# A hybrid trunk on one core: blocks of four third and last, the first tile's products at once, gates spread into the last combination, router products in two halves of the array

## The chip, the cores and the metric

One core of a Trainium2 chip runs the whole program. The metric is the time of one execution on the device, in microseconds (us). The engines are TensorE (PE in the profile; PEld is its weight loading), VectorE (DVE), ScalarE (ACT), GpSimd (POOL) and SyncE (SP), whose queue issues nearly all loads.

## The reference

Two layers over 512 tokens of width 1024, batch 1, all in float32:

```python
for i in range(DEPTH):
    h = _rms_norm(x, norm_mix[i])
    z = h @ w_in[i]
    ...
    x = x + merged @ w_out[i]
    h2 = _rms_norm(x, norm_ffn[i])
    x = x + _hier_moe(h2, ...)
    g_ple = jax.nn.sigmoid(_rms_norm(x, norm_ple[i]) @ w_ple_gate[i])
    x = x + g_ple * (p[i] @ w_ple_proj[i])
return _rms_norm(x, norm_final)
```

Between `z` and `merged` stand dilated attention and a convolution branch. `_hier_moe` chooses one of 4 groups and then 2 of its 8 experts for each token; an expert is `(silu(x @ w_gate) * (x @ w_up)) @ w_down` with a hidden width of 512, and there are 32 of them, each with three matrices of 2 MB.

## The kernel before, in words

The tokens stand in four tiles of 128 rows, `self.x[0..3]`. A layer runs through four parts.

**Mixer.** Products with dense weights are made of three matmuls (`mm3`, L312 to L314): weights and activations are split into a high and a low part. A weight chunk of 128 x 1024 is loaded (`load_chunks`, L216), its high part is made by ScalarE (L234), its low part by GpSimd (L239), or, for the first four chunks and some others, half by GpSimd and half by VectorE (L237). `take(c)` sees to it that chunks up to `c + self.ahead` are split and chunks up to `c + self.look` are loaded. The part starts with the value projection, `tokens_b` over chunks v0 to v3: for each token tile t, `token_b` makes 8 x 3 matmuls (two k for each chunk). Ahead of that the tiles are normalized and transposed: `prep` multiplies x by the row's scale and a gain on VectorE and puts the transposition on the list `todo`; `split_T` transposes a tile on PE (L419), copies the high part on ScalarE (L424) and makes the low part on VectorE (L426). At the program's start (`run`) the loop over t does `rms`, `prep` and `split_chunks(t)`, and pops a transposition at t = 1 and t = 2; what is left is popped by `value`, behind each tile's products. Instructions of this opening are recorded under L102. Behind it come the convolution, attention and output products (ps_z, ps_ao, ps_wo).

**Router.** `route_tile` (one generator for each tile, interleaved with the output products) normalizes and transposes a tile (L832), makes its 36 logits as eight products of 128 x 128 into rows 0 to 35 of a PSUM tile (L841), copies them (L868), transposes them back (L873) and works out the chosen experts on VectorE (L881 to L924). `order_experts` counts tokens for each expert and ranks the 28 experts that are not static by that count.

**Experts.** Tokens are gathered into blocks of 128 slots; a block holds two experts of 64 slots or four of 32. `BLK` lists the blocks: 0 and 1 hold the static experts 0 to 3, the others hold experts by rank, the eight of lowest rank in two blocks of four. Stages c = 0 to 6 take two blocks each. A stage makes, on PE: gate and up products (ps_g, ps_u) of its two blocks, the down products (ps_y) of the blocks of the stage before, transposes (ps_hT), the gathering of the next stage's tokens (ps_xg) and the combination (ps_c) of the blocks two stages back, whose sums VectorE adds to x (L1150). Weights come in items of 512 KB, 384 of them a layer: four of each matrix of an expert. SP issues them (L252) in the order of `self.items`, which `Trunk.__init__` builds from BLK: for c from 1 on, gate and up items of blocks 2c and 2c+1, and, from c = 2, down items of blocks 2c-2 and 2c-1; the down items of blocks 12 and 13 end the list. They land in a ring of 45 slots, `s4`, that is shared with chunks and other rows; `pump` issues items as long as a stage's reserve (`KEEP`) stays free. Behind block 4's gate and up products stands the check for overflowing experts (`overflow`, L1291): a loop whose count is read from memory by every engine.

**Gate.** With the last combination (blocks 12 and 13), `then(t)` transposes tile t of x (L1266) and `first(t)` makes the products with the gate weights pg0 to pg3 (ps_tb). `rms` (squares on ScalarE, L384; a dozen operations on single columns, L392 to L401) and `gated` (tanh L1412, L1414, L1416) stand behind them, and the second half of the products and the next layer's normalization (L431) follow.

Of the kernel before, what the change touches and what calls it, by code (L numbers as in the profile page):

```python
# [8 lines left out]
F32 = mybir.dt.float32  # L9
# [3 lines left out]
AF = mybir.ActivationFunctionType  # L13
OP = mybir.AluOpType
# [3 lines left out]
T, D, P = 512, 1024, 128  # L18
NT = T // P
KD = D // P  # L20
H, HD = 8, 64
CW, CK = 512, 31
NG, NPG, NE = 4, 8, 32
# [3 lines left out]
CAP = 64  # L27
GS = 256


NST, NSM = 4, 8
NDY = NE - NST
LD = 4
BLK = ([(2 * i, 2 * i + 1) for i in range(NST // 2)]
       + [tuple(range(NST + 4 * i, NST + 4 * i + 4)) for i in range(NSM // 4)]
       + [(i, i + 1) for i in range(NST + NSM, NE, 2)])
NB = len(BLK)

# [41 lines left out]
AH = 4  # L80
LK = 5, 3
# [82 lines left out]
class Trunk:  # L164
# [198 lines left out]

    def tokens_b(self, cs, src, then):
        for c in cs:
            self.take(c)
        for t in range(NT):
            then(t, self.token_b(cs, src, t))

# [65 lines left out]
    def run(self):  # L435
# [6 lines left out]
        for t in range(NT):  # L442
            if t:
                nc.sync.dma_start(self.x[t], self.dr["x"][t * P:(t + 1) * P])
            self.load_chunks(t)
        self.small(0)
# [8 lines left out]
        for t in range(NT):  # L455
            n = self.s4.get(F32, "n")
            self.prep(t, gain, self.rms(t, n), n)
            if t in (1, 2):
                self.todo.pop(0)()
            self.split_chunks(t)  # L460
        self.nc = nc
# [29 lines left out]
    def mixer(self, l):  # L491
        nc = self.nc
        v, act = nc.vector, nc.scalar
        base = l * NCH
        self.look, self.ahead = LK[0], AH
        pos = self.pos = {s: base + i for i, s in enumerate(SEQ_CHUNKS)}
# [7 lines left out]
        def value(t, ps):  # L504
            act.activation(vt(t), ps, AF.Copy)
            self.ps.free()
            if self.todo:
                self.todo.pop(0)()
        self.tokens_b([pos[f"v{i}"] for i in range(4)], self.hT, value)

        if l:
            self.load_c2()
# [296 lines left out]
    def route_init(self):  # L809
        self.nh = [[None] * NT for _ in range(2)]  # L810
        self.lgw, self.Ew, self.lgT = (self.s2.get(F32, n) for n in ("lgw", "Ew", "lgT"))
        self.Mb = self.tn(128, "Mb", BF)
        self.spos8, self.base8, self.slots8 = (self.tn(2 * NT, n) for n in ("sp", "sb", "sl"))
# [8 lines left out]
    def route_tile(self, t):  # L822
# [16 lines left out]
        def logits(h):  # L839
            for k in range(4 * h, 4 * h + 4):  # L840
                pe.matmul(pl[0:36, 0:P], self.gwr[:, k * 36:(k + 1) * 36], nT[h][:, k % 4 * P:(k % 4 + 1) * P],  # L841
                          start=k == 0, stop=k == KD - 1)
            self.s2.free()
# [22 lines left out]
        logits(1)  # L866
        lgT = self.lgT[0:36, t * P:(t + 1) * P]
        act.activation(lgT, pl[0:36, 0:P], AF.Copy)  # L868
        self.ps.free()
        for _ in range(LAGS[2]):  # L870
            yield
        pl = self.ps.get(F32, "lg")
        pe.transpose(pl[:, 0:36], lgT, self.cc(C_ID, P)[0:36, 0:36])  # L873

# [57 lines left out]
    def order_experts(self):  # L932

        v = self.nc.vector
        cnt = self.posb[:, 128:160]
        key, rank, small, base, self.cnt, top, rest, bs = (self.lgT[:, 32 * i:32 * i + 32] for i in range(8))
        bs, ss = bs[:, :8], bs[:, 8:16]
        over = lambda a, n: a.unsqueeze(1).to_broadcast([P, n, 32])
# [18 lines left out]
        v.tensor_scalar(small, rank, float(NSM), 32.0, op0=OP.is_lt, op1=OP.mult)  # L957
        v.scalar_tensor_tensor(base, rank, float(NSM - 1), small, op0=OP.subtract, op1=OP.mult)
        v.scalar_tensor_tensor(base, rank, float(CAP), base, op0=OP.mult, op1=OP.subtract)
        if CAP * NST != CAP // 2 * NSM:  # L960
            v.tensor_scalar(base, base, float(CAP * NST - CAP // 2 * NSM), None, op0=OP.add)
        v.tensor_copy(base[:, :NST], self.cc(C_BASE, NST))
# [70 lines left out]
    def moe(self, l):  # L1033
# [219 lines left out]
        cs = [self.pos[f"pg{i}"] for i in range(4)]  # L1253
        self.pg = []

        def first(t):
            self.pg.append(self.token_b(cs, self.src, t))

        def then(t):
# [11 lines left out]
            self.gT[0].append(hi)  # L1271
            self.gT[1].append(lo)
            if t:
                first(t - 1)
        combine((NB - 2, NB - 1), then)
        first(NT - 1)
        for t in range(NT):
            junk = self.s4.get(F32, "j")
            r = self.rms(t, junk)
            self.s4.free()  # L1280
            h_ = self.tn(1, f"rh{t}")
            v.tensor_scalar(h_, r, 0.5, None, op0=OP.mult)
            self.rh.append(h_)

# [116 lines left out]


    def ple(self, l):
        nc = self.nc
# [4 lines left out]

        def gated(t, h, ps):  # L1410
            th = self.s2.get(F32, "th")
            self.last = act.activation(th, ps, AF.Tanh, scale=self.rh[t]).ins  # L1412
            self.ps.free()
            v.scalar_tensor_tensor(th, th, 1.0, self.pp[h](t), op0=OP.add, op1=OP.mult)  # L1414
            xs = self.x[t][:, h * T:(h + 1) * T]
            self.last_v = v.tensor_add(xs, xs, th).ins  # L1416
            self.s2.free()

        for t in range(NT):
            gated(t, 0, self.pg[t])  # L1420
        self.pp[0].free()
# [136 lines left out]
```

## Time and profile before

| | us |
|---|---|
| median of 3 runs | 1818.47 (1818.14 to 1821.3) |
| the profiled execution | 1818.76 |
| its span, first to last instruction | 1817.0 |
| TensorE busy | 1720.2 |
| VectorE busy | 874.1 |
| ScalarE busy | 540.2 |
| GpSimd busy | 380.7 |

The mean granted clock of TensorE was 0.986 of full speed, and the DMA engines moved 478.66 MB. The profile's page gives busy times, the span in slices and the costliest groups of instructions; the trace behind it gives timelines of an engine, the chain of waits (what released each step, followed back from the end), waits by engine, and busy times in any stretch. Layer 0 lasts to about 912 us, layer 1 from there on.

### The profile page before, as it was taken

The page shows a single profiled execution, that of the slowest core. Times are in us where ns is not written, and L with a number is a line of the kernel's source. Part 1 is how long each engine was busy: PE and PEld are TensorE (multiplying, and loading weights), DVE is VectorE, ACT ScalarE, POOL GpSimd, SP SyncE. Part 2 cuts the span into 40 slices and gives each one's busy share as a digit, 9 for nine tenths or more (in the row PEclk, how much of TensorE's full clock was granted, in tenths as well). Part 3 has the DMA queues.
Part 4 walks back from the last instruction along what each step waited for, and adds up shares of the span by engine and source line. Part 5 has one row for each costly group of instructions (what it writes and reads, how often), then busy time and mean ns, then how long its engine had stood idle before and what let it go on. Part 6 is the DMA issues. An engine that isn't in the chain of part 4 may idle for free.

```text
span 1817.0 us, 24202 instructions
## 1 busy us (share of the span) xinstructions
PE 1720.2 (95%) x8324; PEld 1050.6 (58%) x8324; DVE 874.1 (48%) x2131; ACT 540.2 (30%) x1041; POOL 380.7 (21%) x203
## 2 busy tenths in 40 slices
PE   5999999998989999998999999998989899999997
PEld 4777787753244355444777777877514344355356
DVE  5688864572042243223648888537601332343146
ACT  4355534221011012103545554433201011022145
POOL 3445424300200001001444454252002000010021
PEclk9999999999999999999999999999999999999999
DMA  5222236389989999996242212564899899999931
GB/s 228 83 68 71 82 135 236 121 318 387 419 337 419 419 419 416 413 419 275 90 132 70 70 58 70 197 220 174 328 398 419 335 418 419 419 417 419 420 153 47
DMA packets 133616, 478.66 MB, mean 263 GB/s; under 512 B 14832, under 2 KB 15344, under 8 KB 133488
## 3 DMA queue, kind: packets, MB, share of 16 engines
q1 hardware_dynamic: 133488, 477.06, 67.5%
q8 instruction: 68, 1.11, 0.2%
q14 instruction: 60, 0.49, 0.1%
HBM read 474.90 MB, written 2.10 MB: 263 GB/s over the span
## 4 chain that ended last, share of the span: by engine, by line
PE 64%; DMA 20%; DVE 7%; issue 4%; ACT 2%; POOL 1%; SPq 0%; POOLq 0%; DVEq 0%; ACTq 0%
DMA s_w<-wdn 10%; PE ps_g L102 8%; PE ps_y L102 7%; DMA s_w<-wu 6%; PE ps_u L102 6%; PE ps_z L312 6%; PE ps_z L313 6%; PE ps_z L314 6%; PE ps_xg L102 5%; PE ps_c L102 5%; DMA s_w<-wg 3%; PE ps_tb L312 2%; PE ps_tb L313 2%; PE ps_tb L314 2%; PE ps_O L691 1%
## 5 line engine op out<-in xcount | busy, mean ns | idle before, releaser
L239 POOL TENSOR_TENSOR s_lo<-s_raw,s_hi 128x1024 fp32r<-128x1024 f32 x114 | 275.8, 2431 | 811.7 <-ACT s_hi L234 422.7
L102 PE MATMUL ps_u<-s_w,s_xg 128*64 128x512 f32 (+1 forms) x1024 | 240.1, 595 | 12.5 <-DMA s_w<-wu 12.1
L102 PE MATMUL ps_g<-s_w,s_xg 128*64 128x512 f32 (+1 forms) x1024 | 223.4, 603 | 14.2 <-DMA s_w<-wdn 9.3
L102 PE MATMUL ps_y<-s_w,s_hT 128*64 128x512 f32 (+1 forms) x1024 | 223.7, 601 | 11.3 <-DMA s_w<-wdn 10.7
L313 PE MATMUL ps_z<-s_hTl,s_hi 128*128 128x512 f32 x512 | 203.3, 397 | 0.0
L312 PE MATMUL ps_z<-s_hTh,s_hi 128*128 128x512 f32 x512 | 200.1, 391 | 0.0
L314 PE MATMUL ps_z<-s_hTh,s_lo 128*128 128x512 f32 x512 | 199.7, 390 | 0.0
L102 PEld LDWEIGHTS ps_u<-s_w,s_xg 128*64 128x64 f32 (+1 forms) x1024 | 67.7, 130 | 179.3 <-issue 117.3
L102 PEld LDWEIGHTS ps_y<-s_w,s_hT 128*64 128x64 f32 (+1 forms) x1024 | 69.6, 131 | 162.7 <-issue 113.8
L102 PEld LDWEIGHTS ps_g<-s_w,s_xg 128*64 128x64 f32 (+1 forms) x1024 | 64.8, 131 | 160.5 <-issue 127.6
L525 DVE SCALAR_TENSOR_TENSOR s_acc<-ps_z,smt,s_acc 128x511 f32<-128x511 f32 (+27 forms) x210 | 153.8, 732 | 4.6
L234 ACT ACTIVATE s_hi<-s_raw 128x1024 fp32r<-128x1024 f32 x120 | 125.5, 1057 | 8.6 <-PE ps_wo L313 4.2
L1105 DVE SCALAR_TENSOR_TENSOR s_h<-s_h,ps_g 128x512 f32<-128x512 f32 x28 | 19.2, 687 | 210.4 <-ACT s_h L1104 204.0
L1104 ACT ACTIVATE s_h<-ps_g,rs 128x512 f32<-128x512 f32 x28 | 19.2, 686 | 328.4 <-PE ps_g L102 287.7
L1150 DVE TENSOR_TENSOR s_x<-s_x,ps_c 128x512 f32<-128x512 f32 x112 | 75.2, 685 | 79.9 <-PE ps_c L102 47.4
L313 PEld LDWEIGHTS ps_z<-s_hTl,s_hi 128*128 128x128 f32 x512 | 96.2, 188 | 21.9 <-issue 3.1
L312 PEld LDWEIGHTS ps_z<-s_hTh,s_hi 128*128 128x128 f32 x512 | 96.1, 188 | 21.1 <-issue 1.0
L314 PEld LDWEIGHTS ps_z<-s_hTh,s_lo 128*128 128x128 f32 x512 | 96.2, 188 | 19.6 <-issue 0.8
L102 PE MATMUL ps_xg<-s_OH,s_xh 128*128 128x256 f32 x412 | 102.6, 290 | 3.7 <-DVE s_lgT L941 3.7
L1115 ACT ACTIVATE s_hT<-ps_hT 128x512 f32<-128x512 f32 x28 | 15.4, 596 | 300.3 <-PE ps_hT L102 300.3
L102 PE MATMUL ps_xg<-s_OH,s_xl 128*128 128x256 f32 x412 | 101.3, 286 | 0.0
L1106 DVE TENSOR_TENSOR s_h<-s_h,ps_u 128x512 f32<-128x512 f32 x28 | 19.3, 688 | 156.6 <-PE ps_u L102 156.6
(274 smaller groups left out, 2769.8 us busy)
## 6 DMA issues: line engine op xcount, KB each, us to landing
s_w<-wu SPq DMA_DIRECT2D x256, 512.0 KB, 9.9
s_w<-wdn SPq DMA_DIRECT2D x256, 512.0 KB, 9.9
s_w<-wg SPq DMA_DIRECT2D x248, 512.0 KB, 9.9
s_raw<-wd SPq DMA_DIRECT2D x124, 512.0 KB, 3.4
s_w<-wg SPq DMA_DIRECT2D x16, 256.0 KB, 7.4
s_x<-x SPq DMA_DIRECT2D x4, 512.0 KB, 9.9
out<-s_n SPq DMA_DIRECT2D x8, 256.0 KB, 2.0
s_gain<-gains SPq DMA_DIRECT2D x3, 512.0 KB, 3.8
```

The costliest lines, as they stand in the source:

```text
L102: i = f(*a, **k)
L234: nc.scalar.activation(hi, raw, AF.Copy)
L239: nc.gpsimd.tensor_tensor(lo, raw, hi.bitcast(F32), op=OP.subtract)
L312: mm(out, lh, rh, start=start, stop=False)
L313: mm(out, lh, rl, start=False, stop=False)
L314: mm(out, ll, rh, start=False, stop=stop)
L525: v.scalar_tensor_tensor(o, i, w, o, op0=OP.mult, op1=OP.add)
L691: nc.tensor.matmul(ps[64 * hh:64 * hh + 64, j * P:T], vt(j, (2 * p + hh) * HD, (2 * p + hh + 1) * HD), src, start=j == 0, stop=j == 3)
L1104: act.activation(t, pg, AF.Tanh, scale=rh[p])
L1105: v.scalar_tensor_tensor(t, t, 1.0, pg, op0=OP.add, op1=OP.mult)
L1106: v.tensor_mul(t, t, pu)
L1150: v.tensor_add(xs, xs, ps)
```

## The change

- `BLK`: block 2 holds four experts (ranks 0 to 3), blocks 3 to 12 two each, block 13 four (ranks 4 to 7). `order_experts` computes the base slots for this numbering with three more operations on 128 x 32 elements. Stage 1 has then 48 items of gate and up instead of 64, stage 2 loads 24 down items instead of 32, and the last stage loads 16 + 32 gate and up items and 16 + 24 down items.
- Start: tile 0's transposition is popped in the loop at t = 0; those of tiles 1 to 3 are popped by a hook in the middle (after k = 3) of the tile before. Chunks 0, 2, 3 are split by tiles 0, 1, 2, and in layer 0's value projection `ahead` is 1 instead of `AH`.
- Router: products of even k go to rows 0 to 35, those of odd k to rows 64 to 99 of the PSUM tile, that is to two halves of the array's columns; two copies take them out, and two accumulating products with columns of the identity, instead of one transposition, add and transpose them. Rows 32 to 63 of `lgT` are zeroed once a layer.
- Gate: `rms` of tile t moves into `then(t)`, the first half's `gated` into `first(t)`, behind tile t's products.

```diff
-BLK = ([(2 * i, 2 * i + 1) for i in range(NST // 2)]
-       + [tuple(range(NST + 4 * i, NST + 4 * i + 4)) for i in range(NSM // 4)]
-       + [(i, i + 1) for i in range(NST + NSM, NE, 2)])
+BLK = ([(2 * i, 2 * i + 1) for i in range(NST // 2)] + [tuple(range(NST, NST + 4))]
+       + [(i, i + 1) for i in range(NST + NSM, NE, 2)] + [tuple(range(NST + 4, NST + NSM))])
...
-    def tokens_b(self, cs, src, then):
+    def tokens_b(self, cs, src, then, hook=None):
...
-            then(t, self.token_b(cs, src, t))
+            then(t, self.token_b(cs, src, t, hook))
...
-            if t in (1, 2):
+            self.split_chunks((0, 2, 3, 3)[t])
+            if t == 0:
                 self.todo.pop(0)()
-            self.split_chunks(t)
...
-        self.look, self.ahead = LK[0], AH
+        self.look, self.ahead = LK[0], AH if l else 1
...
-            if self.todo:
+            if l and self.todo:
                 self.todo.pop(0)()
-        self.tokens_b([pos[f"v{i}"] for i in range(4)], self.hT, value)
-
+        halves = []
+
+        def middle():
+            halves.append(0)
+            if not l and len(halves) % KD == KD // 2 and self.todo:
+                self.todo.pop(0)()
+        self.tokens_b([pos[f"v{i}"] for i in range(4)], self.hT, value, middle)
+
+        self.ahead = AH
...
+        self.nc.gpsimd.memset(self.lgT[32:64, :], 0.0)
...
-                pe.matmul(pl[0:36, 0:P], self.gwr[:, k * 36:(k + 1) * 36], nT[h][:, k % 4 * P:(k % 4 + 1) * P],
-                          start=k == 0, stop=k == KD - 1)
+                o = k % 2 * 64
+                pe.matmul(pl[o:o + 36, 0:P], self.gwr[:, k * 36:(k + 1) * 36], nT[h][:, k % 4 * P:(k % 4 + 1) * P],
+                          start=k < 2, stop=k >= KD - 2)
...
-        lgT = self.lgT[0:36, t * P:(t + 1) * P]
-        act.activation(lgT, pl[0:36, 0:P], AF.Copy)
+
+        halves = [slice(64 * i, 64 * i + 36) for i in range(2)]
+        lgT = self.lgT[:, t * P:(t + 1) * P]
+        for a in halves:
+            act.activation(lgT[a], pl[a, 0:P], AF.Copy)
...
-        pe.transpose(pl[:, 0:36], lgT, self.cc(C_ID, P)[0:36, 0:36])
+        for i, a in enumerate(halves):
+            pe.matmul(pl[:, 0:36], lgT[0:100], self.cc(C_ID, P)[0:100, a], start=i == 0, stop=i == 1)
...
-        v.scalar_tensor_tensor(base, rank, float(NSM - 1), small, op0=OP.subtract, op1=OP.mult)
+
+        v.tensor_scalar(bs32, rank, 4.0, -40.0, op0=OP.is_ge, op1=OP.mult)
+        v.scalar_tensor_tensor(bs32, bs32, -11.0, rank, op0=OP.add, op1=OP.add)
+        v.tensor_mul(base, bs32, small)
...
-        self.pg = []
-
         def first(t):
-            self.pg.append(self.token_b(cs, self.src, t))
+            self.gated(t, 0, self.token_b(cs, self.src, t))
...
             self.gT[1].append(lo)
+            junk = self.s2.get(F32, "j")
+            r = self.rms(t, junk)
+            self.s2.free()
+            h_ = self.tn(1, f"rh{t}")
+            v.tensor_scalar(h_, r, 0.5, None, op0=OP.mult)
+            self.rh.append(h_)
             if t:
                 first(t - 1)
```

The loop over t with `rms` behind `first(NT - 1)` and the one with `gated(t, 0, ...)` at the head of `ple` are gone; `gated` itself is the same.

Three places of the order. First ScalarE at the start of the program, one piece of the difference; s_n_131 and s_n_149 are tile 1's squares in the one and the other order, ps_tr_149 and ps_tr_131 tile 0's transposes.

```order
-L102 ACTIVATE s_n_131,ss_1_132<-s_x_68 128x512
-L102 ACTIVATE s_n_131,ss_1_134<-s_x_68 128x512
-L102 ACTIVATE s_hTh_100<-ps_tr_149 128x2x128
-L102 ACTIVATE s_hTh_101<-ps_tr_149 128x2x128
-L102 ACTIVATE s_hTh_102<-ps_tr_158 128x2x128
-L102 ACTIVATE s_hTh_103<-ps_tr_158 128x2x128
+L102 ACTIVATE s_hTh_100<-ps_tr_131 128x2x128
+L102 ACTIVATE s_hTh_101<-ps_tr_131 128x2x128
+L102 ACTIVATE s_hTh_102<-ps_tr_140 128x2x128
+L102 ACTIVATE s_hTh_103<-ps_tr_140 128x2x128
+L102 ACTIVATE s_n_149,ss_1_150<-s_x_68 128x512
+L102 ACTIVATE s_n_149,ss_1_152<-s_x_68 128x512
```

Tile 1's squares moved behind the four copies of tile 0's transposes.

Second PE in the last stage of layer 0, where block 12 ends (ps_u) and block 13 begins (ps_g). Before:

```order
L102 MATMUL ps_u_6218<-s_w_6027,s_xg_6058 64x512
L102 MATMUL ps_g_6327<-s_w_6033,s_xg_6057 64x512
L102 MATMUL ps_g_6327<-s_w_6035,s_xg_6057 64x512
L102 MATMUL ps_g_6327<-s_w_6033,s_xg_6057 64x512
L102 MATMUL ps_g_6327<-s_w_6035,s_xg_6057 64x512
```

With the change:

```order
L102 MATMUL ps_u_6134<-s_w_5934,s_xg_5974 64x512
L102 MATMUL ps_g_6243<-s_w_5940,s_xg_5973 32x512
L102 MATMUL ps_g_6243<-s_w_5951,s_xg_5973 32x512
L102 MATMUL ps_g_6243<-s_w_6139,s_xg_5973 32x512
L102 MATMUL ps_g_6243<-s_w_6141,s_xg_5973 32x512
```

Block 13 takes four items (s_w) of four experts in turn, 32 slots each, where it took two of two experts.

Third VectorE in the last combination of layer 0, from the first half of tile 1's sum (s_x_3970 before, s_x_3909 after) on. Before:

```order
L1150 TENSOR_TENSOR s_x_3970<-s_x_3970,ps_c_6638 128x512
L237 TENSOR_TENSOR s_lo_6590<-s_raw_6521,s_hi_6589 128x512
L1268 TENSOR_TENSOR s_gTl_6609<-ps_tr_6610,s_gTh_6608 128x512
L1268 TENSOR_TENSOR s_gTl_6609<-ps_tr_6617,s_gTh_6608 128x512
L1150 TENSOR_TENSOR s_x_3970<-s_x_3970,ps_c_6644 128x512
```

With the change:

```order
L1168 TENSOR_TENSOR s_x_3909<-s_x_3909,ps_c_6669 128x512
L392 TENSOR_SCALAR rms_6655<-ss_0_6651 128x1
L1168 TENSOR_TENSOR s_x_3909<-s_x_3909,ps_c_6675 128x512
L237 TENSOR_TENSOR s_lo_6602<-s_raw_6517,s_hi_6601 128x512
L394 TENSOR_SCALAR rms_6655<-ss_0_6653,rms_6655 128x1
L396 TENSOR_SCALAR rms_6655<-rms_6655 128x1
L397 TENSOR_SCALAR rms_6655<-rms_6655 128x1
L1284 TENSOR_TENSOR s_gTl_6621<-ps_tr_6622,s_gTh_6620 128x512
L1284 TENSOR_TENSOR s_gTl_6621<-ps_tr_6629,s_gTh_6620 128x512
```

The second half of tile 1's sum moved ahead of the split (L237), and the root mean square of tile 0 stands between.

## Rows read from the trace of the kernel before

**Rows 1.** Page, busy time by engine: us (share) x instructions.
```profile
PE 1720.2 (95%) x8324; PEld 1050.6 (58%) x8324; DVE 874.1 (48%) x2131; ACT 540.2 (30%) x1041; POOL 380.7 (21%) x203
```

**Rows 2.** Busy times by stretch; the last columns are clock, DMA share, GB/s.
```profile
core 0: us, PE busy (x) PEld busy (x) DVE busy (x) ACT busy (x) POOL busy (x), PEclk, DMA share, GB/s
50.00:260.00 210.00, 208.85 (x976) 162.15 (x976) 165.72 (x321) 105.35 (x208) 93.11 (x55) 1.00 0.21 69
425.00:485.00 60.00, 51.68 (x198) 9.22 (x191) 4.68 (x11) 1.37 (x2) 3.83 (x2) 1.00 1.02 411
530.00:535.00 5.00, 0.61 (x4) 0.00 (x0) 0.69 (x1) 0.00 (x0) 0.00 (x0) 1.00 0.67 274
540.00:545.00 5.00, 5.00 (x26) 1.72 (x24) 0.13 (x1) 0.69 (x1) 0.00 (x0) 1.00 1.01 402
550.00:555.00 5.00, 5.00 (x46) 1.38 (x46) 0.95 (x2) 0.00 (x0) 0.00 (x0) 1.00 1.03 421
760.00:830.00 70.00, 67.95 (x344) 35.02 (x341) 17.78 (x32) 13.80 (x26) 0.00 (x0) 1.00 1.03 419
830.00:840.00 10.00, 10.00 (x39) 6.91 (x40) 5.72 (x9) 0.00 (x0) 0.00 (x0) 0.85 1.02 419
```

**Rows 3.** Timeline of SP's queue, layer 0's last stage: start us, us, what.
```profile
750.12 9.12 SPq L252 DMA_DIRECT2D s_w<-wg  x8
...
791.34 39.15 SPq L252 DMA_DIRECT2D s_w<-wdn  x32
```

**Rows 4.** Page, DMA issues: count, KB each, us from issue to landing.
```profile
s_w<-wdn SPq DMA_DIRECT2D x256, 512.0 KB, 9.9
```

**Rows 5.** Chain of waits, 755 to 865 us: start us, us, what.
```profile
763.43 7.67 PE ps_xg L102 x64
...
778.37 5.44 PE ps_pe L102 x24
...
811.43 13.73 PE ps_y L102 x64
...
829.61 8.46 PE ps_c L102 x29
838.06 13.93 PE ps_y L102 x64
```

**Rows 6.** Timeline of SP's queue, layer 1's last stage.
```profile
1685.39 39.65 SPq L252 DMA_DIRECT2D s_w<-wdn  x32
```

**Rows 7.** Chain of waits, 1690 to 1750 us.
```profile
1732.38 13.94 PE ps_y L102 x64
```

**Rows 8.** Timeline of PE at the start; in brackets idle before and releaser.
```profile
10.68 1.94 PE L419 MATMUL ps_tr<-c,s_n 128*128 128x128 f32 x8 [10.68 <-DVE s_n L102]
17.88 1.94 PE L419 MATMUL ps_tr<-c,s_n 128*128 128x128 f32 x8 [5.26 <-DVE s_n L102]
...
23.98 1.10 PE L419 MATMUL ps_tr<-c,s_n 128*128 128x128 f32 x8
...
34.74 0.80 PE L313 MATMUL ps_tb<-s_lo,s_hTh 128*128 128x512 f32 x1 [2.25 <-DVE s_lo L102]
...
48.69 0.39 PE L312 MATMUL ps_z<-s_hTh,s_hi 128*128 128x512 f32 x1
```

**Rows 9.** Chain of waits, 5 to 52 us.
```profile
15.61 2.13 DVE s_n L102
```

**Rows 10.** Chain of waits in the router, 318 to 385 us.
```profile
357.18 1.87 PE ps_lg L841 x16
...
367.04 0.28 ACT s_lgT L868
367.37 0.32 PE ps_lg L873
```

**Rows 11.** Waits of PE, 850 to 960 us: total, times, longest.
```profile
PE ps_tr L1266 <- DVE s_x L1150: 3.0, 3, 2.5
PE ps_tr L419 <- DVE s_n L431: 2.5, 2, 2.2
```

**Rows 12.** Chain of waits at the end of layer 1.
```profile
1807.02 0.70 ACT s_th L1412
```

More of the change, by code (lines that the diff above doesn't have):

```diff
@@ L444, in run @@
                 nc.sync.dma_start(self.x[t], self.dr["x"][t * P:(t + 1) * P])
-            self.load_chunks(t)
+            if t < 3:
+                self.load_chunks(t)
+        self.load_chunks(3)
         self.small(0)
@@ L936, in order_experts @@
         key, rank, small, base, self.cnt, top, rest, bs = (self.lgT[:, 32 * i:32 * i + 32] for i in range(8))
+        bs32 = rest
         bs, ss = bs[:, :8], bs[:, 8:16]
@@ L957, in order_experts @@
         v.tensor_scalar(small, rank, float(NSM), 32.0, op0=OP.is_lt, op1=OP.mult)
-        v.scalar_tensor_tensor(base, rank, float(NSM - 1), small, op0=OP.subtract, op1=OP.mult)
+        v.tensor_scalar(bs32, rank, 4.0, -40.0, op0=OP.is_ge, op1=OP.mult)
+        v.scalar_tensor_tensor(bs32, bs32, -11.0, rank, op0=OP.add, op1=OP.add)
+        v.tensor_mul(base, bs32, small)
         v.scalar_tensor_tensor(base, rank, float(CAP), base, op0=OP.mult, op1=OP.subtract)
-        if CAP * NST != CAP // 2 * NSM:
-            v.tensor_scalar(base, base, float(CAP * NST - CAP // 2 * NSM), None, op0=OP.add)
+        v.tensor_scalar(base, base, -128.0, None, op0=OP.add)
         v.tensor_copy(base[:, :NST], self.cc(C_BASE, NST))
@@ L1276, in moe @@
         first(NT - 1)
[L1277 to L1283, printed above, removed]
     def overflow(self, l):
@@ L1400, in overflow, with gated @@
             self.s4.used, self.s2.used, self.ps.used = was
+    def gated(self, t, h, ps):
+        nc = self.nc
+        th = self.s2.get(F32, "th")
+        self.last = nc.scalar.activation(th, ps, AF.Tanh, scale=self.rh[t]).ins
+        self.ps.free()
+        nc.vector.scalar_tensor_tensor(th, th, 1.0, self.pp[h](t), op0=OP.add, op1=OP.mult)
+        xs = self.x[t][:, h * T:(h + 1) * T]
+        self.last_v = nc.vector.tensor_add(xs, xs, th).ins
+        self.s2.free()
     def ple(self, l):
@@ L1408, in ple @@
         last = l == self.L - 1
[L1410 to L1420, printed above, removed]
+        gated = self.gated
         self.pp[0].free()
```

## The prediction

> **What bounds the kernel now.** The page comes first: TensorE is busy 1720.2 us of the 1817.0 us span [rows 1]. That is a mean over stages with different limits, so the table by stretch is next [rows 2]. In the mixer (50 to 260 us) PE is busy 208.85 of 210 us: what starts it earlier ends it earlier. In 760 to 830 the DMA moves 419 GB/s and PE is busy 67.95 of 70 us: two engines near their limits, and the order of the loads decides which ends last. The load queue's timeline tells where that stream ends [rows 3]: in stage 6 of layer 0 the gate and up weights begin at 750.12, and the last 32 items, the down weights of blocks 10 to 13, are issued from 791.34 on for 39.15 us, which is 39.15 / 31 = 1.26 us an item. A load lands 9.9 us after its issue [rows 4], so the last lands near 791.34 + 39.15 + 9.9 = 840.4. The chain of waits holds the decisive reading [rows 5]: PE comes to the last two blocks' down products only at 838.06 and computes them until 851.99, 11.6 us after all data is there. It ran on from 763.43 to 825.2 without a wait. Layer 1 repeats it [rows 6, 7]: the last landing is at 1685.39 + 39.65 + 9.9 = 1734.9, the products end at 1732.38 + 13.94 = 1746.3, 11.4 us later. So at the end of the experts PE is behind the DMA, although earlier (425 to 485 us, 51.68 us busy of 60 at 411 GB/s) PE waited for the data [rows 2].
>
> **Blocks.** Bytes and items stay the same, only their order moves. A four-expert block has twice the items of a pair and the same PE time: 46 of its products stand in 5 us where 26 of a pair do [rows 2], so one takes half the time. Before, both such blocks stand at the start of the dynamic part, where PE waits for data anyway. After, one of them ends that part: the down weights of blocks 10 and 11 are followed by 8 + 16 items instead of 8 + 8, and all of stage 6 loads 88 items instead of 64. Working backwards from the last landing at 840.4, blocks 10 and 11 have their weights by 840.4 - 24 x 1.26 = 810.2; their last products and the combination of 8.46 us [rows 5] are over by about 822, and the down products of block 12 (8 items) and block 13 (16 items) then follow as the items land. The last item feeds a few products, some 0.5 us. So these products end near 840.9 and not at 851.99: 11.1 us; in layer 1 near 1735.4 and not at 1746.3: 10.9. I subtract 0.5 us in each, since PE comes into the last combination from a stretch paced by loads, and the combination that now follows such waits (830 to 840) had a granted clock of 0.85 [rows 2]. Taken: **21 us** for both layers. Bounds: 22 (nothing subtracted), and 18 if each layer's stream loses 2 us more. The middle stages have cover: a stage loads 48 items, 60.5 us at 1.26, and PE's part of it is 825.2 - 763.43 - 5.44 + 1 = 57.3 us [rows 5]. Two stages have 5.44 us of embedding products on top and lag by 2 us each; the longer last stage takes that up. The three new operations for the base slots stand once a layer on VectorE: nothing.
>
> **Start.** PE transposes tiles 0 and 1 before any product, the first at 10.68, the second at 17.88 after 5.26 us of idle; another wait is 2.25 us for a split, and the first product of the next phase stands at 48.69 [rows 8]. After, tile 0's products follow its own transposes, which end at 10.68 + 1.94 = 12.6. If PE never waited again, 96 products of 5.44 / 24 = 0.227 us [rows 5] and the transposes of three tiles at 1.10 [rows 8] would end at 12.6 + 21.8 + 3.3 = 37.7, a gain of 11.0. But the rest of chunk 1's split stands on VectorE behind tile 1's normalization (2.13 us [rows 9]), whose squares are now behind the copies of tile 0 on ScalarE: by that order these products start near 19.9, while chunk 0's six are over at about 15. 4.5 us stay, and I add 1 for the copies between: 43.2, so **5.5 us**, with 0 and 8.5 as bounds. The splits that are put off (one ahead instead of four) fall on ScalarE and GpSimd, busy 105.35 and 93.11 of 210 us in the mixer [rows 2]. If that cover fails, PE waits for one of them as it did for the split here, 2.25 us.
>
> **Router.** Eight products of a tile's router take 1.87 us [rows 10]. In two halves of the array they could take half, 0.94. Against that stand a second transposition product (the one that is there takes 0.32) and, on the last tile, a second copy (0.28). A layer's four tiles save 3.7 and pay up to 1.6, and of the three early tiles a part goes to waits on VectorE instead. I take 1 us a layer, **2 us**; bounds 5 and -1. The position products that move behind the gathering stay off the logits' path, and the memset runs once a layer on GpSimd, idle there: nothing. Do halves run side by side at all? The tiles of two and four experts in one PSUM bank do: 26 products in 5 us for one kind, 46 for the other [rows 2]. The Trainium skill, in TensorEngine Tiling (Array Packing), section Restrictions and Gotchas, says that different row tiles cannot access the same PSUM bank simultaneously; if that held for these column halves too, which both write one bank, the router would gain nothing and the sum would lose this term. The trace's 46 against 26 speaks against it for columns.
>
> **Gating.** At the layers' boundary PE waits 3.0 us for combined rows and 2.5 us for the next layer's normalized rows [rows 11]. The root mean squares and the gates of the first half stand there in one lump on VectorE; spread through the combination, they are done when the next layer's rows are due. The new order also puts the second half of tile 1's addition ahead of a split, which takes most of the 3.0 us wait. But the squares now stand on ScalarE ahead of the last weights' splits, and PE may wait for those instead, once 2.25 us as at the start [rows 8] or a little less. **2 us**; bounds 5.5 and -1.5. In layer 1 the tail behind the last product begins at 1807.02 [rows 12] and has no lump ahead of it: nothing.
>
> **Sum.** 21 + 5.5 + 2 + 2 = 30.5 us. The profiled execution took 1818.76 us (span 1817.0, 1.76 around it), 0.29 above the median of the three runs. 1818.76 - 30.5 = 1788.3: I say **1788 us**. All terms at their good ends: 1777.8; all at their bad ends: 1803.3.
>
> **Rivals.** *The end is not won.* At the third stage's overflow check PE is busy 0.61 of 5 us (530 to 535) and the stream falls to 274 GB/s [rows 2]. After, the check comes 16 items earlier in the stream. If each layer's stream loses some 10 us there or by full buffers, the end is where it was: 1788 + 21 = 1809. For it: loads share their slots with everything else. Against it: PE waits for data just before, so in both orders it comes to the check with nothing in reserve.
> *Slower.* Its place is the ring of slots in stages 3 to 6, its price the bandwidth that is lost while the queue waits for a slot. Before, the last loads had 11 us of slack; after, they end the part, and each lost us counts. It decides from 15.3 us a layer (30.5 / 2). A dip like the one at 530 costs 5 x (1 - 274 / 419) = 1.7 us; it would need two to three of these in each of four stages, some 18 us a layer: 1788 + 36 = 1824. Against it: the stretch 760 to 830, made of such stages, runs at 419 GB/s.
> *Halves one after the other.* By the rule above, worked with rows: the router keeps 1.87 us a tile and pays about 1 us a layer: 1788 + 2 + 2 = 1792.
> *The start gives nothing,* because VectorE's chain sets it: 1793.5.
>
> **How the numbers follow.** Forecast 0.62, the end not won 0.18, slower 0.07, halves in sequence 0.08, start nothing 0.05. The range begins near the forecast's good end and reaches over the last two into the first rival: 1779 to 1807. About 0.2% (3.6 us) is what a measurement of this kernel can tell from no change. A quarter of the first rival falls within it: faster 0.88, same 0.05, slower 0.07.
>
> **What would show it.** Down products that end within 1.5 us of the last landing; a first product of the second phase near 43; a tile's router products in about 1 us; no 2.5 us wait for combined rows. The prediction is wrong if the stream has new dips, if PE still ends the experts with 13.9 us of products without waits, or if the last combination takes 5 us longer than before.

## The result, and the profile after

The changed kernel took 1795.51 us, median of 4 runs (1794.73 to 1796.25), against 1819.27 of the kernel before in the same comparison (4 runs): a ratio of 0.9868 with a 95% interval of 0.9851 to 0.9885, some 24 us less. That lies inside the forecast range of 1779 to 1807 and 7.5 us over the forecast of 1788. The gain is smaller than the 30.5 us forecast; one of the four terms came out with the other sign.

The page's first row after, to be held against [rows 1]: the span fell by 22.5 us and PE's busy time by 15.

```profile
span 1794.5 us, 24263 instructions
...
PE 1705.2 (95%) x8348; PEld 1045.9 (58%) x8348; DVE 882.8 (49%) x2137; ACT 543.5 (30%) x1049; POOL 380.9 (21%) x205
```

The load queue's timeline in layer 0's last stage (start us, us, what) answers to [rows 3]: now 16 of each for block 13, then 40 down items.

```profile
737.68 19.40 SPq L252 DMA_DIRECT2D s_w<-wg  x16
757.65 19.63 SPq L252 DMA_DIRECT2D s_w<-wu  x16
778.19 49.61 SPq L252 DMA_DIRECT2D s_w<-wdn  x40
```

The chain of waits of the same stage answers to [rows 5]. Where PE ran 763.43 to 825.2 without a wait, the chain now passes through loads.

```profile
764.87 7.08 PE ps_g L102 x64
771.95 9.87 DMA s_w<-wu
...
802.63 8.38 DMA s_w<-wdn
...
813.84 6.89 PE ps_c L102 x29
820.73 6.75 PE ps_y L102 x31
827.47 9.87 DMA s_w<-wdn
837.39 1.91 PE ps_y L102 x10
839.29 2.15 PE ps_c L1165 x8
```

The last down item is issued until 778.19 + 49.61 = 827.8 and lands at 837.3 by the chain. The products end at 839.29, 2 us behind it, where the prediction looked for at most 1.5. In layer 1 the same rows, against [rows 6, 7], first the queue, then the chain:

```profile
1661.31 50.20 SPq L252 DMA_DIRECT2D s_w<-wdn  x40
```

```profile
1704.98 6.19 PE ps_y L102 x28
1711.17 9.83 DMA s_w<-wdn
1721.05 1.90 PE ps_y L102 x10
1722.95 2.16 PE ps_c L1165 x8
```

**Where the time went.** Marks in each trace split the span into pieces: the first ps_z product, the last start of an output product (ps_wo) in a layer, the first dynamic load, the end of the last down loads' issue, the end of the last down products, the first ps_z of layer 1, the end. Each piece is a difference of two rows of a timeline; the unit is us, L0 and L1 are the layers. The last two columns count from the end of the last down product, in layer 0 and in layer 1.

| run | first ps_z | last ps_wo to first dynamic load, L0 / L1 | last down issue to last down product, L0 / L1 | from there to layer 1's first ps_z | L1: last down product to the end |
|---|---|---|---|---|---|
| before | 48.69 | 66.0 / 67.3 | 21.5 / 21.2 | 89.8 | 70.7 |
| the change | 44.25 | 67.5 / 69.5 | 11.5 / 11.4 | 87.1 | 71.6 |
| no_router | 44.24 | 65.9 / 66.5 | 11.5 / 11.4 | 87.1 | 69.9 |
| no_blocks | 44.69 | 66.5 / 67.9 | 21.5 / 21.8 | 85.6 | 70.0 |
| no_start | 49.20 | 67.9 / 67.9 | 11.5 / 11.4 | 85.6 | 69.9 |
| no_gate | 43.41 | 67.9 / 68.1 | 11.5 / 11.4 | 89.7 | 68.8 |
| blocks_only | 49.94 | 67.5 / 67.3 | 11.5 / 11.4 | 89.8 | 70.5 |
| router_only | 48.45 | 70.7 / 68.1 | 20.0 / 21.4 | 89.7 | 70.5 |
| gate_layer0 | 44.00 | 67.9 / 66.7 | 11.5 / 11.5 | 87.1 | 70.5 |
| mask_one_input | 43.30 | 66.0 / 65.8 | 11.5 / 11.4 | 88.3 | 71.5 |
| xl_halves | 43.70 | 66.7 / 65.5 | 11.5 / 11.5 | 85.5 | 70.0 |
| mask_halves | 45.34 | 64.5 / 65.4 | 11.5 / 11.4 | 88.4 | 69.9 |

By the first two rows, each one profiled execution: start -4.4, router (the third column) +1.5 and +2.2, blocks -10.0 and -9.8, gates -2.7 in layer 0 and +0.8 in layer 1; the stream from the first dynamic load to the last issue is 436.7 us in each layer after and was 436.8 and 437.1, so it has no new dip. With 0.4 us that the mixer of layer 0 took back these pieces make the 22.5 us by which the span fell.

**The router's piece.** Here lies the miss. The chain of waits of the change in layer 0's router answers to [rows 10]:

```profile
350.15 2.38 DVE Mb L916
...
354.23 1.00 PE ps_lg L852 x16
...
356.13 0.41 PE ps_lg L888 x4
...
360.87 0.41 PE ps_lg L852 x2
361.28 0.12 PE ps_pos L931
361.40 0.87 PE ps_lg L852 x6
362.29 0.27 ACT s_lgT L882
362.58 0.28 ACT s_lgT L882
362.90 1.07 PE ps_lg L888 x4
```

The products themselves do what was forecast in this layer: 1.00 us a tile instead of 1.87. But a new stretch of 2.38 us stands in VectorE's addition into Mb (the mask of the two chosen experts), which the kernel before made in 0.19. PE's waits for it, here in layer 1 (total, times, longest):

```profile
PE ps_pos L931 <- DVE Mb L916: 3.0, 1, 3.0
```

GpSimd's timeline of layer 0 shows what ran then: the split of tile 2's rows begins 0.03 us ahead of the addition and ends within 0.06 us of it (350.12 + 2.35 = 352.47; 350.15 + 2.38 = 352.53).

```profile
350.12 2.35 POOL L871 TENSOR_TENSOR s_xl<-s_x,s_xh 128x1024 fp32r<-128x1024 f32 x1 [6.86 <-ACT s_xh L870]
```

In the kernel before, the same two stood the other way round; the first three rows are VectorE's timeline, the last GpSimd's.

```profile
355.28 0.19 DVE L901 TENSOR_TENSOR Mb<-s_Ew 128x32 bf16<-128x32 f32 x1
...
356.04 0.18 DVE L922 SCALAR_TENSOR_TENSOR s_lgw<-s_Ew,ps_pos 128x32 f32<-128x32 f32 x1
...
356.16 1.78 DVE L924 SCALAR_TENSOR_TENSOR sl<-sp,sb,sl 128x1 f32<-128x1 f32 x1
```

```profile
355.54 2.38 POOL L860 TENSOR_TENSOR s_xl<-s_x,s_xh 128x1024 fp32r<-128x1024 f32 x1 [7.13 <-ACT s_xh L859]
```

There the addition began 0.26 us before the split and was done in 0.19; the operation held up was a slot computation (L924, to 357.94; the split ends at 357.92), for which PE doesn't wait at that point. With the new router the addition slips behind the split's start; which of its parts (the shorter products, the second copy or the second transposition product) shifts it was not tested.

PE's waits for Mb ahead of the gathering grow from 0.7 to 3.0 us in both layers, yet layer 1 pays more than layer 0. What differs is the granted clock behind the wait. Busy times by stretch (start:end, us, PE busy, clock, DMA share, GB/s), the change in layers 0 and 1, then the kernel before in layer 1:

```profile
353.60:358.60 5.00, 5.00 (x37) 1.00 0.82 231
1235.30:1240.30 5.00, 5.00 (x29) 0.66 0.73 203
```

```profile
1250.70:1255.70 5.00, 4.83 (x28) 1.00 0.97 331
```

In the second stretch the new products of that tile took 1.86 us at a granted clock of 0.66, as long as the old ones at 1.00.

The third column also holds more than PE's path. SP's queue issued the ten static down items ahead of the first dynamic load in 12.31 us instead of 11.10 in layer 0; these rows are of the change and of the kernel before:

```profile
377.88 12.31 SPq L252 DMA_DIRECT2D s_w<-wdn  x10
```

```profile
381.65 11.10 SPq L252 DMA_DIRECT2D s_w<-wdn  x10
```

Measured to the gathering's first product instead, from the last start of ps_wo, the change pays 0.2 us in layer 0 and 2.2 in layer 1. By that mark the old router takes 39.2 to 40.1 us in its six layers (before, no_router, blocks_only) and the new one, with Mb and the split as they are in the change, 40.2 to 42.5 in its twelve. The ranges don't meet. The mean granted clock of these stretches is 0.96 to 1.00 with the old router and 0.91 to 0.97 with the new one, and the longest of the new ones are those with the lowest clock. At an equal mean of 0.96 or 0.97 the new router is 0.2 to 0.8 us longer.

**The gates' piece.** Waits of PE, 830 to 960 us, against [rows 11]:

```profile
PE ps_tr L1282 <- DVE s_x L1168: 2.8, 3, 1.5
...
PE ps_tb L314 <- DVE s_gTl L1284: 0.8, 1, 0.8
```

The wait for normalized rows (2.5 us) is gone; the one for combined rows fell only from 3.0 to 2.8 in all, its longest part from 2.5 to 1.5.

**The start's piece.** Timeline of PE with idle time and releaser, against [rows 8]:

```profile
9.91 1.94 PE L419 MATMUL ps_tr<-c,s_n 128*128 128x128 f32 x8 [9.91 <-DVE s_n L102]
...
13.27 0.63 PE L314 MATMUL ps_tb<-s_hi,s_hTl 128*128 128x512 f32 x1
13.70 0.63 PE L312 MATMUL ps_tb<-s_hi,s_hTh 128*128 128x512 f32 x1
...
16.26 0.80 PE L313 MATMUL ps_tb<-s_lo,s_hTh 128*128 128x512 f32 x1 [0.56 <-POOL s_lo L102]
...
18.58 1.33 PE L419 MATMUL ps_tr<-c,s_n 128*128 128x128 f32 x5 [0.67 <-DVE s_n L102]
...
23.62 0.39 PE L313 MATMUL ps_tb<-s_lo,s_hTh 128*128 128x512 f32 x1
23.85 0.39 PE L314 MATMUL ps_tb<-s_hi,s_hTl 128*128 128x512 f32 x1
...
44.25 0.39 PE L312 MATMUL ps_z<-s_hTh,s_hi 128*128 128x512 f32 x1
```

The waits of 5.26 and 2.25 us are gone, and the first ps_z comes 4.4 us sooner. Five waits stay behind tile 0's transposes, of 0.35 to 0.67 us, 2.35 together. Up to about 23.2 one product follows another after 0.43 us (13.27 to 13.70), from there after 0.23 (23.62 to 23.85).

### The profile page after: what moved, and what is told of

It is laid out like the page before. It is cut to its first block, busy times and chain, and to the rows that moved or that the text cites. A ratio compares the mean times of both kernels' runs of the same rounds, so it can differ in the third digit from the quotient of the medians.

```text
span 1794.5 us, 24263 instructions
## 1 busy us (share of the span) xinstructions
PE 1705.2 (95%) x8348; PEld 1045.9 (58%) x8348; DVE 882.8 (49%) x2137; ACT 543.5 (30%) x1049; POOL 380.9 (21%) x205
## 4 chain that ended last, share of the span: by engine, by line
PE 68%; DMA 16%; DVE 7%; issue 5%; ACT 2%; POOL 1%; SPq 0%; POOLq 0%; DVEq 0%; ACTq 0%
PE ps_g L102 9%; DMA s_w<-wdn 8%; PE ps_u L102 7%; PE ps_y L102 7%; PE ps_xg L102 6%; DMA s_w<-wu 6%; PE ps_z L312 5%; PE ps_z L313 5%; PE ps_z L314 5%; PE ps_c L102 5%; PE ps_tb L312 3%; PE ps_tb L314 3%; PE ps_tb L313 3%; POOL s_lo L239 1%; PE ps_pe L102 1%
## 5 line engine op out<-in xcount | busy, mean ns | idle before, releaser
L102 PE MATMUL ps_y<-s_w,s_hT 128*64 128x512 f32 (+1 forms) x1024 | 227.4, 601 | 9.0 <-DMA s_w<-wdn 8.3
L102 PE MATMUL ps_g<-s_w,s_xg 128*64 128x512 f32 (+1 forms) x1024 | 206.8, 603 | 13.2 <-issue 6.6
```

The costliest lines, as they stand in the source:

```text
L102: i = f(*a, **k)
```

## The experiments

Four runs undo one part each, three do one part or a piece of it, three test the cause that the router's piece suggested. All ratios are against the kernel before on the same chip; the change itself stands at 0.9868 [0.9851, 0.9885].

**Router undone (no_router).**

```diff
-                o = k % 2 * 64
-                pe.matmul(pl[o:o + 36, 0:P], self.gwr[:, k * 36:(k + 1) * 36], nT[h][:, k % 4 * P:(k % 4 + 1) * P],
-                          start=k < 2, stop=k >= KD - 2)
+                pe.matmul(pl[0:36, 0:P], self.gwr[:, k * 36:(k + 1) * 36], nT[h][:, k % 4 * P:(k % 4 + 1) * P],
+                          start=k == 0, stop=k == KD - 1)
...
-        for i, a in enumerate(halves):
-            pe.matmul(pl[:, 0:36], lgT[0:100], self.cc(C_ID, P)[0:100, a], start=i == 0, stop=i == 1)
+        pe.transpose(pl[:, 0:36], lgT, self.cc(C_ID, P)[0:36, 0:36])
```

> The change with the router as it was (eight products in one half, one copy, one transposition). Theory, lock: the new router moves VectorE's addition into Mb under GpSimd's split of tile 2's rows, and PE waits 3.0 us for it in each layer. Undone, the addition takes 0.2 us again, the wait for Mb is under 1 us a layer, a tile's products take 1.87 us again, and the time is 1792 to 1794, that is 1.5 to 3.5 us under the change. Rival, halves pay: the shorter products gain and the wait comes from the earlier start: then the wait of 3 us stays and the time is 1797 or more.

1792.32 us (1789.77 to 1793.8), ratio 0.9864 [0.9845, 0.9882]. That is within the expected 1792 to 1794, but by time alone it can't be told from the change. By the trace it can: the router's piece is 65.9 and 66.5 us instead of 67.5 and 69.5, and no Mb takes more than 0.193 us. Layer 0's waits of PE (318 to 384 us) have lost the 3.0:

```profile
PE ps_pos L925 <- DVE Mb L910: 0.7, 2, 0.5
```

In layer 1 a wait of 2.4 us in three parts stays, as in the kernel before, so "under 1 us a layer" was too low there; its longest part, 1.7, is the last tile's and stands behind the start of the gathering. With the old router Mb isn't held up, and the way to the gathering is shorter.

**Blocks undone (no_blocks).**

```diff
-BLK = ([(2 * i, 2 * i + 1) for i in range(NST // 2)] + [tuple(range(NST, NST + 4))]
-       + [(i, i + 1) for i in range(NST + NSM, NE, 2)] + [tuple(range(NST + 4, NST + NSM))])
+BLK = ([(2 * i, 2 * i + 1) for i in range(NST // 2)]
+       + [tuple(range(NST + 4 * i, NST + 4 * i + 4)) for i in range(NSM // 4)]
+       + [(i, i + 1) for i in range(NST + NSM, NE, 2)])
...
```

(and the base slots as before)

> The change with the two blocks of four in second and third place of the dynamic part, as before. Theory, PE behind the stream at the end: the last down products run 13.9 us without waits and end some 11.5 us after the last landing, in both layers; the time is 1815 to 1816.5. Rival, the order only moves dips of the stream: the end of the down products moves by less than 7 us a layer and the time is under 1810.

1812.76 us (1810.67 to 1815.3; the kernel before 1817.98 there), ratio 0.9975 [0.9964, 0.9987]. The blocks are worth 0.9975 - 0.9868 = 1.07%, 19.5 us. The down products again end 21.5 and 21.8 us behind the last issue, in one run without waits (chain of waits):

```profile
834.88 13.93 PE ps_y L103 x64
```

The median is 2 us under the expected 1815 to 1816.5, as is that chip's median of the kernel before by 1.3.

**Start undone (no_start).**

```diff
-            self.split_chunks((0, 2, 3, 3)[t])
-            if t == 0:
+            if t in (1, 2):
                 self.todo.pop(0)()
+            self.split_chunks(t)
...
```

(and `ahead`, the transpositions behind a tile's products and the empty hook as before)

> The change with the old opening (two tiles transposed first, one chunk split with each tile, four chunks ahead). Theory: the first product of the second phase is back at 48.7 instead of 44.25 and the mixer passes it on: 1799 to 1800. Rival: the mixer or the router takes it back by waits: under 1798.

1798.85 us (1796.21 to 1801.16), ratio 0.9901 [0.9883, 0.992]: just under the expected 1799 to 1800. The part is worth 0.33%, 6 us with a 95% uncertainty of some 4.5 us. The trace has the first ps_z at 49.20 and the old 2.25 us wait back. The old opening's price reaches the end, though its size is uncertain.

**Gates undone (no_gate).**

```diff
-            self.gated(t, 0, self.token_b(cs, self.src, t))
+            self.pg.append(self.token_b(cs, self.src, t))
```

(and the loops behind the combination as before)

> The change with the root mean squares and the first half's gates in one lump behind the last combination. Theory: layer 0's boundary loses 2.6 us and layer 1's end gains 0.9: 1796.5 to 1798, with a wait of 2 us or more for the next layer's normalized rows. Rival, the boundary's gain comes from the earlier last landing alone: within 0.5 us of the change, no such wait.

1795.53 us (1791.29 to 1798.01), ratio 0.9877 [0.9853, 0.9901]: under the expected 1796.5 to 1798, and not to be told from the change by time. In the trace layer 0's boundary takes 89.7 us instead of 87.1, and PE's waits there are those of [rows 11] again:

```profile
PE ps_tr L1284 <- DVE s_x L1168: 3.0, 3, 2.5
PE ps_tr L419 <- DVE s_n L431: 2.4, 2, 2.2
```

The rival, a gain from the earlier landing alone, had no such wait and falls. Over all runs the boundary is 89.7 to 89.8 with the lump (four runs) and 85.5 to 88.4 without (eight): the part gains 1.3 to 4.3 us in layer 0. The spread of the eight is the granted clock of the boundary: a mean of 1.00 where it took 85.5 or 85.6 us, 0.98 where 87.1, 0.96 where 88.3 or 88.4, with the same waits of PE. The boundaries with the lump have 0.98; at that clock the part gains 2.7 us.

**Gates spread in layer 0 alone (gate_layer0).**

```diff
+        spread = l < self.L - 1
...
-            self.gated(t, 0, self.token_b(cs, self.src, t))
+            ps = self.token_b(cs, self.src, t)
+            if spread:
+                self.gated(t, 0, ps)
+            else:
+                self.pg.append(ps)
```

> The change with the gates spread through the last combination in layer 0 alone, in one lump in layer 1 as before. Theory, the spread gates help where normalization for a next layer follows and cost where none follows: from the end of the down products to the end of the program 69 instead of 71.5 us, layer 0's boundary at 85.5 to 87.1 us; 0.5 to 2.5 us under the change. Rival: layer 1's tail doesn't care: within 0.5 us of the change.

1792.61 us (1791.79 to 1796.19), ratio 0.9864 [0.9838, 0.989]: no difference by time. Layer 1's end takes 70.5 us with the lump; over all runs it is 68.8 to 70.7 with it and 69.9 to 71.6 without. My reading that spreading costs in layer 1 isn't borne out: the two overlap.

**Blocks alone on the kernel before (blocks_only).**

```diff
-BLK = ([(2 * i, 2 * i + 1) for i in range(NST // 2)]
-       + [tuple(range(NST + 4 * i, NST + 4 * i + 4)) for i in range(NSM // 4)]
-       + [(i, i + 1) for i in range(NST + NSM, NE, 2)])
+BLK = ([(2 * i, 2 * i + 1) for i in range(NST // 2)] + [tuple(range(NST, NST + 4))]
+       + [(i, i + 1) for i in range(NST + NSM, NE, 2)] + [tuple(range(NST + 4, NST + NSM))])
...
```

(and the base slots as in the change)

> The kernel before with the new order of blocks alone. Theory: the end of the down products 11.5 us after the last issue instead of 21.5 in both layers, and nothing else: 19 to 21 us under the kernel before. Rival: part of the gain needs the gates in the combination, since the last weights' splits come sooner after the last landing: 16 us or less.

1800.04 us (1799.03 to 1801.04) against 1818.7, ratio 0.9899 [0.9876, 0.9923]: 18.4 us, with both ends at 11.5 us. That is the 19 to 21 expected within the interval, and the rival's 16 lies inside the interval's edge (0.9923 is 14 us); the trace decides for the first, since the two ends move by 10 us each as in the change and the boundary stays at 89.8.

**Router alone on the kernel before (router_only).**

```diff
-                pe.matmul(pl[0:36, 0:P], self.gwr[:, k * 36:(k + 1) * 36], nT[h][:, k % 4 * P:(k % 4 + 1) * P],
-                          start=k == 0, stop=k == KD - 1)
+                o = k % 2 * 64
+                pe.matmul(pl[o:o + 36, 0:P], self.gwr[:, k * 36:(k + 1) * 36], nT[h][:, k % 4 * P:(k % 4 + 1) * P],
+                          start=k < 2, stop=k >= KD - 2)
...
```

(and the copies, the transposition products and the zeroed rows as in the change)

> The kernel before with the router's halves alone. Theory, lock: logits of a tile in 1.0 instead of 1.87 us, Mb 2.4 us once a layer, PE waits 3.0 us for it; from the last output products to the first gate product 1 to 2 us longer in layer 0 and no shorter in layer 1; time 0 to 4 us over the kernel before. Rival: halves pay when the opening is the old one: 2 us or more under it.

1819.89 us (1811.54 to 1821.84, 10 runs) against 1818.7 (13 runs), ratio 1.0001 [0.9984, 1.0017]. No gain shows in time, though the interval would still allow one of 3 us. Mb takes 2.373 us at its longest here too, and the router's piece is 4.7 us longer in layer 0, more than the expected 1 to 2, and 0.8 in layer 1. The excess in layer 0 goes with the clock again: 0.53 granted from 357.4 to 362.4 us, behind the wait. So the hold-up belongs to the new router and not to the earlier start.

**Mb from one compare (mask_one_input).**

```diff
-        v.tensor_tensor(mb(t), E[0], E[1], op=OP.add)
+        v.tensor_scalar(mb(t), lem, v2, None, op0=OP.is_ge)
```

> The change with one VectorE operation replaced: Mb, the mask of the two chosen experts, comes from one compare of one row block (lem >= v2) instead of the sum of two. Theory, lock: an operation with two inputs in SBUF waits as long as GpSimd works, one with a single input doesn't: Mb takes about 0.2 us in each of its eight places though GpSimd's split runs beside it, PE's 3.0 us wait for it falls under 1 us, and the time is 2 to 5 us under the change's, against the kernel before 25 to 29 us. Rival, VectorE is slow there for another reason (its output in bf16, or a wait on PSUM): Mb still takes 2.4 us and the wait stays. Second rival: the stretch moves to the next operation with two inputs and PE waits for that one: Mb 0.2 us, time as for the change.

1788.39 us (1786.06 to 1789.65), ratio 0.9832 [0.9808, 0.9856], 30 us under the kernel before where 25 to 29 were expected; the interval overlaps the change's. All eight Mb take 0.234 to 0.236 us, and the router's piece is 66.0 and 65.8 us, shorter than with the old router in layer 1 (66.5 to 67.3). As the second rival had it, the stretch moved to the next operation with two inputs in SBUF, here from VectorE's timeline with GpSimd's below:

```profile
349.32 2.40 DVE L918 SCALAR_TENSOR_TENSOR s_Ew<-s_Ew,c 128x32 f32<-128x32 f32 x1
```

```profile
349.29 2.38 POOL L871 TENSOR_TENSOR s_xl<-s_x,s_xh 128x1024 fp32r<-128x1024 f32 x1 [6.88 <-ACT s_xh L870]
```

It again ends with the split. But PE doesn't wait for this one at once: its longest wait for Mb is 2.2 us instead of 3.0, and falls one tile later, where VectorE's chain comes late; under 1 us was expected. One half of the expectation was not tested here: since the compare doesn't wait for the second choice, the tile's Mb was made from 347.14 on, two us ahead of the split, and not beside it. The kernel before has the case: an operation with one input in SBUF (L923) took 0.15 us at 355.97, inside the split of 355.54 to 357.92.

**The split in two operations (xl_halves).**

```diff
-        nc.gpsimd.tensor_tensor(lo, x, hi.bitcast(F32), op=OP.subtract)
+        for a in (slice(0, T), slice(T, 2 * T)):
+            nc.gpsimd.tensor_tensor(lo[:, a], x[:, a], hi[:, a].bitcast(F32), op=OP.subtract)
```

> The change with GpSimd's split of a tile's rows in the router (128 x 1024, 2.4 us) made as two operations of 128 x 512. Theory, lock: an operation of VectorE with two inputs in SBUF waits for the GpSimd operation that runs, not for the split as a whole; Mb of tile 2 takes at most 1.4 us instead of 2.37, PE's wait for it falls from 3.0 to 2 us or less, and the time is 0.5 to 2 us under the change's. Rival, the wait is for the finished split (an order by semaphore): Mb still 2.4 us and the wait 3.0.

1787.76 us (1787.52 to 1789.12), ratio 0.9838 [0.9816, 0.986], some 5 us under the change and more than was expected, though the two intervals overlap. The hold-up is cut at the border of the two GpSimd operations: VectorE's timeline, then GpSimd's.

```profile
349.41 1.27 DVE L917 TENSOR_TENSOR Mb<-s_Ew 128x32 bf16<-128x32 f32 x1
350.61 1.32 DVE L919 SCALAR_TENSOR_TENSOR s_Ew<-s_Ew,c 128x32 f32<-128x32 f32 x1
```

```profile
349.37 2.50 POOL L872 TENSOR_TENSOR s_xl<-s_x,s_xh 128x512 fp32r<-128x512 f32 x2 [6.52 <-issue]
```

Mb waits for the first half (349.37 + 1.25 = 350.62), the next operation for the second. The rival, a wait for the finished split, would have kept 2.4 us for Mb and falls. PE's wait fell from 3.0 to 1.9. Each stretch is shorter, but there are two of them.

**Both (mask_halves).** The two edits above together.

> The change with both: the mask Mb from one compare, and the split in two operations. Theory: the stretch of the operation behind Mb (2.4 us with the mask alone) falls to 1.4 or less, in each layer; as PE didn't wait for that one for long, the time is 0 to 1.5 us under the mask alone, so 27 to 32 us under the kernel before. Rival: a second GpSimd operation finds a second operation of VectorE to hold up, and it is no better than the mask alone or slower.

1784.65 us (1783.39 to 1789.41, 5 runs), ratio 0.9817 [0.9798, 0.9836]. This beats both kernels: 33 us under the one before, where 27 to 32 were expected, and some 9 under the change (its interval doesn't meet the change's). The operation behind Mb takes 1.30 and 1.31 us in the two layers, as expected, and the router's piece is 64.5 and 65.4 us. That it is better than either edit alone is not shown: those intervals overlap (0.9808 to 0.9856 and 0.9816 to 0.986).

## Why the prediction was right, and where it was off

**Blocks: right.** The step "the end is at the last landing" held: 10.0 and 9.8 us by the trace, 19.5 and 18.4 by time, for 21 forecast; the runs no_blocks and blocks_only show that this term comes from the order alone. The missing 1.2 us is the end itself: the products end 2 us behind the last landing (837.3 to 839.29), where 0.5 and an allowance of 0.5 were taken, while the landing came 9.5 us behind the issue and not 9.9. The rivals of a lost or dipping stream fell: 436.7 us in both layers.

**Start: right in size, in part by luck.** 4.4 us for 5.5, and no_start shows that it reaches the end; over all runs the first ps_z stands at 48.45 to 49.94 with the old opening and at 43.30 to 45.34 with the new one. 43.2 was forecast and 44.25 came, but by two errors that nearly cancel. The waits that stay were put at 5.5 us and measure 2.35. The pace was put at 0.227 us a product throughout; at that pace and without waits the phase would end 25.1 us after tile 0's transposes, at 11.85 + 25.1 = 36.95. Of the 7.3 us from there to 44.25 some 5 are left when the waits are taken off, and they are the slow pace up to 23.2. The profile gives a granted clock of 1.00 from 10 to 25 us, so why PE was slow there is not shown.

**Gates: right in size, by another route.** 2.7 - 0.8 = 1.9 for 2. The wait for the next layer's rows went as forecast; of the wait for combined rows, which was to go for the most part, 2.8 of 3.0 us stay, although the second half of tile 1's addition now stands ahead of a split. The 0.8 in layer 1 is within the spread of the runs. Time alone doesn't show this term.

**Router: wrong in sign.** The step "of the three early tiles a part goes to waits on VectorE" took those waits as they stood. The halves do run side by side, 1.00 us for 1.87, so the rival of halves in sequence fell. But the order of two engines changed: 0.3 us earlier or later decided whether VectorE's addition into Mb came ahead of GpSimd's split or had to sit it out, and PE waits for that addition. Forecast -2, measured +3.7 by the two traces, of which 1.2 are the queue's and not PE's. The hold-up itself is shown: no_router and router_only tie it to the new router, xl_halves to the GpSimd operation that runs. That it costs more than the halves save rests on the traces, where the way to the gathering is longer in all twelve layers with the new router than in all six with the old; the times of no_router and router_only leave both signs open. A part of that cost is the granted clock behind the wait, which the forecast had nowhere. One more term of the router's sum was too small. The last tile's path gained nothing: from its first product to the gathering it takes 363.97 - 360.87 = 3.10 us, before 367.68 - 365.21 = 2.47 by the chain, since the second transposition product costs more than I had (1.07 us for the two there, 0.32 for the one [rows 10]).

A page of the Trainium skill states the rule that I didn't weigh. The Trainium skill, in SBUF — State Buffer, section SBUF: two separate sides, says that VectorE and GpSimd share a pair of ports as an exclusive lock: a VectorE operation with two inputs in SBUF and a GpSimd operation that reads SBUF exclude each other for the whole instruction, and the one that starts first has it. The trace agrees in each case here: 2.38 us for 0.19 beside a split of 2.35, and 1.27 when the split is made of two pieces. It agrees on the condition of two inputs too: in the kernel before a VectorE operation with one input in PSUM (L922) ran its usual 0.18 us at 356.04, inside the split of 355.54 to 357.92.

Still open: why the granted clock fell at the layers' boundary and behind the wait for Mb in some executions and not in others of the same order. Each trace is one profiled execution.

## What to carry to other kernels

Where a stage's end is set by PE while the stream of loads has ended, put the work with most bytes for its PE time last: PE then ends with the stream, here 10 us a layer sooner. Before shortening a step on one engine, look which pair of operations on VectorE and GpSimd stand within a few tenths of a us of each other behind it: swapping them can cost a whole GpSimd operation, here 2.4 us. Cutting the GpSimd operation in two bounded the hold-up of one VectorE operation at 1.27 us here, but the next one was then held up as long. And read the granted clock behind a new wait of PE: the wait is only a part of its price.

## What the runs showed of the hardware

Eight products of 36 columns took 1.87 us into one half of the array's columns and 1.00 us alternating between two halves of one PSUM bank, both at a granted clock of 1.00; at 0.66 the latter took 1.86. Behind a wait of PE of 3.0 us the granted clock was 0.66 in one layer and 1.00 in the other. The hold-up between VectorE and GpSimd lasted to the end of the GpSimd operation: an operation of 0.19 us took 2.38 when it began 0.03 us behind the other engine's, and 0.19 when it began 0.26 us ahead.
